# Product-key routing on Trainium2: the gates' exponentials on ACT, or as powers of e on POOL

## The chip, the cores and the metric

The kernel runs on one core of a Trainium2 chip. The metric is the time of one execution on the device, in microseconds (us); lower is better. The engines are named as in the profile: PE is the matrix engine (TensorE), PEld its weight load, DVE the vector engine, ACT the scalar engine, POOL GpSimd, SP the engine that issues most of the DMAs.

## The reference

Two blocks of a transformer work on 256 tokens of width 1024. The first block has two layers: latent attention and then chunked gated linear attention (`gla`), each followed by a feed-forward layer with product-key retrieval (`peer_ffn`). The second block is a token mixer and a hierarchical mixture of experts. The change lies in the retrieval layer:

```python
def one_block(xi):                                   # 128 tokens
    q = (xi @ w_query).reshape(B, T, 8, 2, 64)
    s = einsum('bthcd,cnd->bthcn', q, sub_keys)      # two halves, 128 keys each
    s_top, i_top = lax.top_k(s, 16)
    cand = s_top[..., 0, :, None] + s_top[..., 1, None, :]
    best, pos = lax.top_k(cand.reshape(..., 256), 16)
    idx = take_along_axis(cand_idx, pos)             # 16 of 16384 rows per head
    gate = softmax(best)
    h = gelu(einsum('bthkd,btd->bthk', u_tab[idx], xi))
    return einsum('bthk,bthkd->btd', gate * h, v_tab[idx])
```

Each token takes 16 rows for each of 8 heads, so 128 rows of `u` and 128 of `v` in each of the two layers. The gate is a softmax over the 16 best sums of a head.

## The kernel before

The program runs its stages one after the other: latent attention, the two retrieval layers with the linear attention between them (`experts`), the mixer, and the mixture of experts. Tiles, semaphores and the order of instructions on each engine are made when the program is built: a planner walks the instructions with a timeline of its own and puts each on its engine's queue when that timeline says it is ready. On the chip every engine works through its queue in that fixed order.

In `experts` there are four passes: layer 0 or 1 (`l`) and token block 0 or 1 (`b`). A pass has 128 gathers of 128 rows each (one row per token): one indirect DMA from POOL (L911) brings, for one of the token's 128 choices, the `u` row and the `v` row, 8 KB per token. Ten buffers (`g`) hold gathers. A slot of the loop is one gather and its work in `meet`: DVE multiplies the `u` half with the token's vector and sums (a dot into `hs`), and for two gathers together ACT takes gelu (L920), DVE multiplies with the gate, ACT makes a diagonal matrix for each (L924), and PE multiplies it with the `v` half into the output sums (L927); after that the buffer is free for a later gather.

The rows of a group of heads are chosen by `route`, whose steps are strewn between the slots of the group before: two matmuls against the keys, top-16 of each half on DVE, the candidate sums, top-16 again, the decoding of the row numbers (`idx`), and the gate. There are 17 groups: the first two have one head, the others two. In the pass of layer 0, block 1 and that of layer 1, block 0, the linear attention of the other token block (`gla`) is also worked in between the slots; it loads its own weights through SP, and takes exponentials, a logarithm and a silu on ACT.

All DVE instructions of `route` and the dots and gate products of `meet` are issued through the wrapper `InOrder` (line L135 in the profile for all of them), which adds a dependence from each to the one before. So they keep the order in which the program names them. DVE work of `gla` does not pass through the wrapper and can stand between.

The steps of the gate, at the end of `route`: DVE subtracts the best sum from all 16 (`gate`), ACT takes the exponential in place (L893), DVE sums it (`sm`), takes the reciprocal and multiplies. The next instruction on that chain is the next dot. ACT holds one table of functions at a time; the program has an ACT_TABLE_LOAD wherever the table changes, and the exponential and gelu are in different ones. Powers on POOL exist already in the kernel: the reciprocal root of each norm is taken as x to the power of -1/2 (`mhalf`, L300, L370, L651, L687 and others).

Of the kernel before, what the change touches and what calls it, by code (L numbers as in the profile page):

```python
# [9 lines left out]
FT = mybir.dt.float32  # L10
# [4 lines left out]
AF = mybir.ActivationFunctionType  # L15
OP = mybir.AluOpType
# [127 lines left out]
class K:  # L144
# [619 lines left out]
    def experts(self):  # L764
        nc, tc = self.nc, self.tc
        mm = nc.tensor.matmul
        y = self.y
        with self.phase("peer", ps=(6, 7), pq=(2, 3)) as mp:
            V = InOrder(tc, nc.vector)
            n_a = [16 // (a + 1) for a in range(16)]  # L770
            offs = np.concatenate([[0], np.cumsum(n_a)])
            NC = int(offs[-1])
            ct = mp.tile([128, 3, 16], FT, name="ct")
            for j in range(1, 16):
                nc.gpsimd.memset(ct[:, 0, j - 1:j], float(offs[j]))
# [51 lines left out]
            def route(l, b, hs):  # L827
                n = len(hs)
# [19 lines left out]
                V.tensor_tensor(dif, tif[:, :, :, 1:16], tif[:, :, :, 0:15], op=OP.subtract)  # L848
                cand = new("cand", NC)
                for a in range(8):  # L850
                    k = n_a[a]
                    V.tensor_tensor(cand[:, :, int(offs[a]):int(offs[a]) + k], top[:, :, 1, 0:k],
                                    top[:, :, 0, a:a + 1].to_broadcast([128, n, k]), op=OP.add)
                V.tensor_tensor(cand[:, :, int(offs[8]):NC], top[:, :, 0, 8:16],
                                top[:, :, 1, 0:1].to_broadcast([128, n, 8]), op=OP.add)
# [34 lines left out]

                sm, gate = new("sm", 1), new("gate", 16, bufs=3)
                V.tensor_tensor(gate, best, best[:, :, 0:1].to_broadcast([128, n, 16]), op=OP.subtract)
                nc.scalar.activation(gate, gate, AF.Exp)  # L893
                V.tensor_reduce(sm, gate, axis=AX.X, op=OP.add)
                V.reciprocal(sm, sm)
                V.tensor_tensor(gate, gate, sm.to_broadcast([128, n, 16]), op=OP.mult)
# [4 lines left out]
            def prepare(l, b, hs):  # L901
                for h in hs:
                    yield from query(l, b, h)
                yield from route(l, b, hs)
# [52 lines left out]
            for j, (l, b, hs) in enumerate(groups):  # L957
# [3 lines left out]
                for _ in dots(batches):  # L961
# [7 lines left out]
                    while plan and slot >= plan[0][0]:  # L969
# [3 lines left out]
                        n = (slot - begin) * parts // max(1, end - begin)  # L973
# [350 lines left out]
    def moe(self, out):  # L1324
        nc, tc = self.nc, self.tc
        y = self.y
        with self.phase("moe", ps=(2, 3, 6, 7)) as mp:
# [134 lines left out]
            def experts(once):  # L1462
                wts = weights(once)
                for q in range(8):
# [58 lines left out]
                    for b in range(2):  # L1523
                        for n in range(2):
                            mm(y[b][n], C[:, b, :], ys[:, n * 512:(n + 1) * 512], start=False, stop=False,
                               skip_group_check=True)

            experts(True)
            fin = self.pp.tile([128, 2, 1024], FT, name="fin", tag="h")
            sq1 = fin[:, 1, 512:640]  # L1530
# [11 lines left out]
            with tc.For_i(1, rounds, 1):  # L1542
                nc.vector.tensor_scalar(rank, rank, -32.0, None, op0=OP.add)
                experts(False)
# [39 lines left out]
```

## Time and profile before

| | before |
|---|---|
| median of 3 runs | 2353.03 us (2347.0 to 2353.46) |
| the profiled execution | 2348.37 us |
| its span, first to last instruction | 2346.6 us |
| mean granted clock of PE in it | 0.966 |
| busy in the span: PE, DVE, ACT, POOL | 2041.3, 1416.9, 714.4, 637.2 us |
| DMA | 849.30 MB, mean 362 GB/s |

The page of the profile gives these sums for the whole span; the stages have different limits, so the windows by stage say more. A line of a group gives the busy time, the mean duration, and the idle time of that engine just before these instructions with what ended it. In a timeline, the bracket at the end of a line is that idle time for one instruction.

### The profile page before, as it was taken

What the parts mean: (1) busy time and instruction counts of PE and PEld (TensorE: products, weight loads), DVE (VectorE), ACT (ScalarE), POOL (GpSimd) and SP (SyncE); (2) the same over time, 40 slices, a digit from 0 to 9 for tenths busy, and PEclk for the clock granted to TensorE, in tenths of its full rate; (3) what the DMA queues carried; (4) which work ended last, traced back from release to release, by engine and by line L of the source; (5) the groups of instructions that cost most, each with busy time, mean ns of one, the idle gap of its engine ahead of it and who ended that gap; (6) DMA issues with size and microseconds to landing.
All of it is one profiled execution on the core that took longest, in us unless ns stands there. A gap on an engine that the chain in (4) does not pass through costs nothing. (4 is left out here: it accounts for less than half of the span.)

```text
span 2346.6 us, 26348 instructions
## 1 busy us (share of the span) xinstructions
PE 2041.3 (87%) x8134; PEld 1068.5 (46%) x8136; DVE 1416.9 (60%) x3813; ACT 714.4 (30%) x1767; POOL 637.2 (27%) x666
## 2 busy tenths in 40 slices
PE   8999877879898888988887777779999989999996
PEld 7775333334444434444443232338899942222221
DVE  7768767778778678768787677556676530000001
ACT  6632222234344224344322222125555410000000
POOL 4124434434434443435344443410000000000000
PEclk9989999999999999999999999999999999999998
DMA  4359999999999999999999999965477699999996
GB/s 157 101 209 401 419 421 421 421 421 421 422 399 388 395 421 421 422 421 420 378 421 421 421 421 421 421 254 173 150 244 252 231 385 417 417 418 417 418 418 278
DMA packets 161210, 849.30 MB, mean 362 GB/s; under 512 B 18308, under 2 KB 18948, under 8 KB 95528
## 3 DMA queue, kind: packets, MB, share of 16 engines
q0 software_dynamic: 73728, 536.90, 55.4%
q1 hardware_dynamic: 87048, 310.12, 34.3%
q8 instruction: 68, 1.11, 0.2%
q14 instruction: 78, 0.64, 0.1%
q10 hardware_dynamic: 288, 0.52, 0.1%
HBM read 846.42 MB, written 1.05 MB: 361 GB/s over the span
## 5 line engine op out<-in xcount | busy, mean ns | idle before, releaser
L927 PE MATMUL ps<-g,dw 128*128 128x512 f32 x2048 | 976.7, 626 | 191.8 <-ACT dw L924 189.7
L911 POOL DMA_INDIRECT g<-in_puv_dram,idx x512 | 575.0, 1123 | 808.1 <-PE ps L927 466.8
L135 DVE CUSTOM_DVE_ANT_0 g<-g,xs 128x1024 f32<-128x1024 f32 x512 | 621.3, 1221 | 176.9 <-DMA g<-in_puv_dram,idx 164.4
L927 PEld LDWEIGHTS ps<-g,dw 128*128 128x128 f32 x2048 | 392.2, 199 | 720.9 <-issue 401.9
L270 DVE TENSOR_TENSOR wl<-raw,wh 128x512 fp32r<-128x512 f32 (+3 forms) x404 | 268.7, 678 | 128.7 <-ACT wh L268 114.2
L268 ACT ACTIVATE wh<-raw 128x512 fp32r<-128x512 f32 (+3 forms) x408 | 242.2, 613 | 135.2 <-PE ps L293 115.8
L920 ACT ACTIVATE w<-hs 128x2 f32<-128x2 f32 x256 | 51.9, 203 | 687.2 <-DVE hs L135 686.9
L1499 PE MATMUL ps<-we,xT 128*32 128x512 f32 x788 | 185.2, 600 | 20.3 <-DMA we<-in_e_gu_dram 20.3
L924 ACT ACTIVATE dw<-ident,w 128x128 f32<-128x128 f32 x512 | 177.4, 393 | 61.6 <-DVE w L135 57.3
L1504 DVE TENSOR_TENSOR hid<-hid,ps 128x512 f32<-128x512 f32 x8 | 5.5, 687 | 246.1 <-PE ps L1499 246.1
L292 PE MATMUL ps<-xH,wh 128*128 128x256 f32 (+1 forms) x456 | 130.6, 286 | 1.1 <-DVE sel L1191 1.1
L294 PE MATMUL ps<-xL,wh 128*128 128x256 f32 (+1 forms) x456 | 130.6, 286 | 0.0
L293 PE MATMUL ps<-xH,wl 128*128 128x256 f32 (+1 forms) x456 | 130.2, 285 | 0.0
L1533 POOL MEMSET fin<- 128x128 f32 x1 | 0.2, 206 | 404.0 <-DMA we<-in_e_gu_dram 404.0
L1499 PEld LDWEIGHTS ps<-we,xT 128*32 128x32 f32 x788 | 35.7, 108 | 159.7 <-DMA we<-in_e_gu_dram 116.1
L1517 PE MATMUL ps<-we,hT 128*32 128x512 f32 x400 | 95.4, 598 | 0.1
L135 DVE TENSOR_TENSOR w<-w,gate 128x2 f32<-128x2 f32 x256 | 41.1, 160 | 87.5 <-ACT w L920 82.5
L292 PEld LDWEIGHTS ps<-xH,wh 128*128 128x128 f32 (+1 forms) x456 | 87.2, 191 | 2.9 <-issue 1.5
L294 PEld LDWEIGHTS ps<-xL,wh 128*128 128x128 f32 (+1 forms) x456 | 87.2, 191 | 1.2 <-issue 1.1
L293 PEld LDWEIGHTS ps<-xH,wl 128*128 128x128 f32 (+1 forms) x456 | 87.3, 191 | 0.7 <-issue 0.6
L292 PE MATMUL ps<-wh,x 128*128 128x512 f32 (+1 forms) x160 | 63.9, 400 | 16.5 <-ACT wh L268 16.1
L294 PE MATMUL ps<-wl,x 128*128 128x512 f32 (+1 forms) x160 | 68.7, 431 | 7.2 <-DVE wl L270 6.3
(452 smaller groups left out, 2438.5 us busy)
## 6 DMA issues: line engine op xcount, KB each, us to landing
we<-in_e_gu_dram SPq DMA_DIRECT2D x197, 512.0 KB
we<-in_e_dn_dram SPq DMA_DIRECT2D x100, 512.0 KB
raw<-in_gla_w_dram SPq DMA_DIRECT2D x48, 512.0 KB
wx<-in_e_gu_dram SPq DMA_DIRECT2D x35, 512.0 KB
raw<-in_pq_dram SPq DMA_DIRECT2D x24, 512.0 KB
raw<-in_mx_conv_dram SPq DMA_DIRECT2D x24, 512.0 KB
raw<-in_e_gu_dram SPq DMA_DIRECT2D x24, 512.0 KB
g<-in_puv_dram,idx POOLq DMA_INDIRECT x512
```

The costliest lines, as they stand in the source:

```text
L135: r = f(*a, **k)
L268: nc.scalar.activation(H[:, :n], src, AF.Copy)
L270: e.tensor_tensor(L[:, :n], src, H[:, :n].bitcast(FT), op=OP.subtract)
L292: mm(out, aH, bH, start=start, stop=False, **kw)
L293: mm(out, aL, bH, start=False, stop=False, **kw)
L294: mm(out, aH, bL, start=False, stop=stop, **kw)
L911: nc.gpsimd.indirect_dma_start(out=g.rearrange("p a b -> p (a b)"), out_offset=None, in_=self.i[f"puv{l}"], in_offset=bass.IndirectOffsetO ...
L920: nc.scalar.activation(w, hs, AF.Gelu)
L924: nc.scalar.activation(d, self.ident, AF.Copy, scale=w[:, k:k + 1])
L927: mm(y[b][n], d, g[:, 1, n * 512:(n + 1) * 512], start=False, stop=left[l, b] == 0, skip_group_check=True)
L1499: mm(p[e * 32:(e + 1) * 32, :], xg[:, c, e * 32:(e + 1) * 32], ws[e][:, u * 512:(u + 1) * 512], start=c == 0, stop=c == 7, skip_group_chec ...
L1517: mm(pd[n][e * 32:(e + 1) * 32, :], hT[:, c, e * 32:(e + 1) * 32], ws[e][:, n * 512:(n + 1) * 512], start=c == 0, stop=c == 3, skip_group_ ...
```

## The change

In `experts`, a tile of one column is filled with e, once. In `route`, the exponential of the gate is no longer an activation on ACT but a two-input operation on POOL: the constant, spread over the tile, to the power of the gate's input. Nothing else is edited; the gelu, and the exponentials, logarithm and silu of `gla`, stay on ACT.

```diff
@@ in experts
             NC = int(offs[-1])
+            self.euler = mp.tile([128, 1], FT, name="euler")
+            nc.gpsimd.memset(self.euler, math.e)
             ct = mp.tile([128, 3, 16], FT, name="ct")
@@ in route
                 V.tensor_tensor(gate, best, best[:, :, 0:1].to_broadcast([128, n, 16]), op=OP.subtract)
-                nc.scalar.activation(gate, gate, AF.Exp)
+                nc.gpsimd.tensor_tensor(gate, self.euler[:, :, None].to_broadcast([128, n, 16]), gate, op=OP.pow)
                 V.tensor_reduce(sm, gate, axis=AX.X, op=OP.add)
```

## Rows read from the trace of the kernel before

**Rows 1.** The changed line, all its instructions.

```profile
L893 ACT ACTIVATE gate<-gate x17: 215/229/231, 151.4 to 1455.0; 128x32 f32<-128x32 f32 x15, 128x16 f32<-128x16 f32 x2
```

**Rows 2.** The routing stage: PE, PEld, DVE, ACT, POOL busy, PEclk, DMA share, GB/s.

```profile
150.00:1550.00 1400.00, 1167.54 (x3136) 550.41 (x3134) 1035.89 (x2755) 432.34 (x1150) 587.13 (x527) 0.95 1.00 414
```

**Rows 3.** Windows around single gates, the same columns.

```profile
225.00:230.00 5.00, 5.00 (x13) 2.28 (x12) 4.46 (x9) 1.79 (x6) 2.59 (x3) 1.00 0.67 224
...
545.00:565.00 20.00, 17.58 (x55) 9.52 (x54) 17.51 (x44) 10.00 (x22) 8.37 (x7) 1.00 1.02 423
...
740.00:760.00 20.00, 17.25 (x56) 9.77 (x56) 18.31 (x40) 10.99 (x27) 8.42 (x6) 0.91 1.00 407
...
1120.00:1140.00 20.00, 15.12 (x33) 6.45 (x32) 16.61 (x37) 8.66 (x19) 5.47 (x5) 0.74 0.79 314
```

**Rows 4.** Groups of DVE in the window 150 to 1550.

```profile
L135 DVE CUSTOM_DVE_ANT_0 g<-g,xs 128x1024 f32<-128x1024 f32 x506 | 613.9, 1221 | 169.4 <-DMA g<-in_puv_dram,idx 159.2 <-PE ps L927 8.2 <-issue 0.8
...
L135 DVE TENSOR_REDUCE sm<-gate 128x2 f32<-128x32 f32 (+1 forms) x17 | 3.1, 184 | 9.2 <-ACT gate L893 9.2
```

**Rows 5.** The gathers' DMA queue on the page (packets, MB, share).

```profile
q0 software_dynamic: 73728, 536.90, 55.4%
```

**Rows 6.** Groups of ACT in the window 150 to 1550.

```profile
L920 ACT ACT_TABLE_LOAD x23 | 29.5, 1283 | 0.4
L893 ACT ACT_TABLE_LOAD x16 | 20.5, 1283 | 0.3
```

**Rows 7.** DVE in order of time (start, duration, instruction, idle before it).

```profile
159.31 1.22 DVE L135 CUSTOM_DVE_ANT_0 g<-g,xs 128x1024 f32<-128x1024 f32 x1
...
221.38 0.18 DVE L135 TENSOR_REDUCE sm<-gate 128x2 f32<-128x32 f32 x1 [3.99 <-ACT gate L893]
...
293.96 0.18 DVE L135 TENSOR_REDUCE sm<-gate 128x2 f32<-128x32 f32 x1 [0.30 <-ACT gate L893]
...
301.28 1.23 DVE L135 CUSTOM_DVE_ANT_0 g<-g,xs 128x1024 f32<-128x1024 f32 x1 [1.16 <-DMA g<-in_puv_dram,idx]
...
1125.86 0.18 DVE L135 TENSOR_REDUCE sm<-gate 128x2 f32<-128x32 f32 x1 [0.72 <-ACT gate L893]
```

**Rows 8.** ACT in order of time.

```profile
289.00 1.28 ACT L893 ACT_TABLE_LOAD   x1
...
293.94 1.28 ACT L920 ACT_TABLE_LOAD   x1
```

**Rows 9.** Groups of POOL in the whole span, by shape.

```profile
L300 POOL TENSOR_TENSOR gst<-gst,mhalf 128x1 f32<-128x1 f32 x8 | 6.9, 864 | 11.0 <-DVE gst L299 10.4 <-DVE w L135 0.6
L651 POOL TENSOR_TENSOR rk<-ss,mhalf 128x16 f32<-128x16 f32 x2 | 5.8, 2922 | 0.1
...
L687 POOL TENSOR_TENSOR rq<-rq,mhalf 128x8 f32<-128x8 f32 x2 | 3.3, 1632 | 0.0
...
L575 POOL TENSOR_TENSOR t<-kr,tabs 128x32 f32<-128x32 f32 x1 | 0.3, 300 | 1.9 <-DVE kr L611 1.9
```

**Rows 10.** Durations of one POOL power (ns: shortest, median, longest).

```profile
L300 POOL TENSOR_TENSOR gst<-gst,mhalf x8: 550/562/1595, 650.0 to 1087.9; 128x1 f32<-128x1 f32 x8
```

**Rows 11.** POOL in order of time.

```profile
152.21 1.23 POOL L911 DMA_INDIRECT g<-in_puv_dram,idx  x1 [20.45 <-DVE gate L135]
...
300.66 0.94 POOL L911 DMA_INDIRECT g<-in_puv_dram,idx  x1 [7.01 <-PE ps L927]
...
556.05 0.95 POOL L911 DMA_INDIRECT g<-in_puv_dram,idx  x1 [9.01 <-DVE hs L135]
...
1135.15 1.27 POOL L911 DMA_INDIRECT g<-in_puv_dram,idx  x1 [11.40 <-PE ps L927]
```

**Rows 12.** L911 alone (POOL) in a window from 150 us.

```profile
150.00:300.60 150.60, 65.96 (x60) 0.93 0.97 399
```

**Rows 13.** Instructions that touch `xs` (PE, PEld, DVE) in that window.

```profile
150.00:300.60 150.60, 0.00 (x0) 0.00 (x0) 66.61 (x55) 0.93 0.97 399
```

**Rows 14.** PE in order of time.

```profile
456.98 3.56 PE L927 MATMUL ps<-g,dw 128*128 128x512 f32 x4 [2.37 <-ACT dw L924]
```

## The prediction, on record before the change was run

> **What bounds the kernel now.** I read the page first, then the windows by stage, then the groups of DVE, ACT and POOL for the routing stage alone, and last the timelines around single gates. The changed line runs 17 times, from 151 to 1455 us of the span [rows 1], all of it in the product-key stage, which lasts from about 150 to 1550 us. There no engine is full: in those 1400 us PE is busy 1168, DVE 1036, POOL 587 and ACT 432, while the DMA share is 1.00 and the rate 414 GB/s [rows 2]; full windows show 420 to 423, as the one from 545 [rows 3]. DVE's dot products wait 159.2 us for gathers to land [rows 4]. So DMA sets this stage: 536.90 MB in 512 gathers [rows 5] are 1.049 MB each, which at 421 GB/s take 2.49 us. The rest of the span is not touched by the edit and moves with the end of this stage. Two questions follow. Relief on ACT buys little where ACT is 31% busy; and any new stop costs only what it starves DMA of.
>
> **What is removed.** On ACT the 17 exponentials at 0.23 us (3.9 us) go, and the 16 table loads of that line at 1.283 us (20.5 us) [rows 6]. With them go those loads of the gelu line that only undo them: 23 loads stand there now; the chunked-attention work behind (exponentials, logarithm, silu in both passes) still forces some 8 or 9 of them, so I take 14 away, 18 us. ACT gets back about 42 us. What of it lies on a path? DVE waited for the gate's exponential 9.2 us in the 17 gates together [rows 4], 3.99 of it at 217, and 0.30 at a quiet gate like that of 293 [rows 7]: the load runs at 289.00, while ACT waits for the gate's input, and the one back to gelu at 293.94 [rows 8], while DVE is at the rest of the gate and the next dot. Outside 217, 645 and 1124 ACT's part is hidden already. I give the relief 1 us.
>
> **What is added.** A POOL power of 128x32 for 15 groups and of 128x16 for the first two. The trace has powers on POOL, of another base and exponent: 128x1 takes 0.55 us undisturbed, 128x8 1.63 us, 128x16 2.92 us [rows 9, 10]. That is a line: (2.92 - 1.63) / 8 = 0.16 us for each column on a base of 0.37 us. So 128x16 costs 2.9 us and 128x32 5.5 us (estimate from that line). The lower bound is the POOL product of 128x32, 0.30 us [rows 9]: it would hold if a power with base e ran like a product. The upper bound takes the same line with the worst disturbance seen of a 128x1 power, 1.60 against 0.55 us [rows 10], so about 6.5 us. I take 5.5, since the rows of the same operation are nearest. The memset of the one-column constant runs once, while POOL waits for the first route.
>
> [...]
>
> **Where it stands in the order.** The routing chain and the dots are issued on DVE through one in-order wrapper, so the sum of the gates (`sm`) and every dot behind it wait for POOL, and nothing of the chain can pass. The wait of 0.30 us becomes about 5.5: **+5.2 us at a full gate**, +2.7 at the two half ones. Added up, 15 x 5.5 + 2 x 2.9 - 9.2 = 79 us of DVE standing still. That is the top of the cost, if none is hidden.
>
> POOL itself loses little: after a full gate it now stands idle about 7 us, waiting for PE to free a gather buffer (7.01 before 300.66 [rows 11]; seven of the eight quiet gates show 6.3 to 7.1), because those buffers need dots that come after the gate. The power fits in that hole. At most one gather of 0.9 to 1.3 us runs ahead of it. So what is late next is the following dot, then gelu, the diagonal, PE's matmuls, the freed buffer, and so the next gather.
>
> **What hides it.** Gathers already issued. At 300.66, when POOL resumes after the gate of 293.7, 60 gathers were issued and 55 dots begun; the 56th dot starts at 301.28 on its landing [rows 7, 12, 13]. The last of the 60 lands 4 transfers later, and a gather in its turn would show its dot at 301.28 + 5 x 2.49 = 313.73. A gather needs 7.1 us from issue to dot (the very first: 152.21 to 159.31) [rows 7, 11], so the one issued at 300.66 could show it at 307.8. The cover is 6.0 us. The same sum at the other seven quiet gates (374, 454, 830 and the four after 1200) gives 4.5 to 6.9. So in these eight groups +5.2 us is just about covered. [...] 6.0 against covers of 4.5 to 6.9 loses about 0.4 each: **3 us**.
>
> The six groups that share the stage with chunked attention (549, 645, 747, 924, 1019, 1124) have its weights in the DMA queues too, so I go by stops of POOL. A stop of 9.01 us before 556 leaves the 20 us window full (423 GB/s), and so does one of the same kind at 924; the one of 11.40 us before 1135 leaves 314, a loss of 20 x (1 - 314/421) = 5.1 us [rows 3, 11]. At 549 and 924 the stop grows to about 14 us: beyond 9, all of 5.2 would be lost, but by the row at 1135 less; half, 2.6 each. At 1124 the sum starts at 1125.86 [rows 7], about 2 us after the gate's input, so +3.4, all lost. At 747 DMA is under full already (407 GB/s) [rows 3]: 5.2. At 645, with a wait like that at 1124 and a full window, 1; at 1019, where POOL stops for 5 us only, nothing. Together **15 us**.
>
> At the start: DMA has nothing else until the first gather at 152.21 [rows 11]; the power (2.9 us) becomes ready just before it, at 151.4 [rows 1], and may go ahead of gathers: 2 us. The group at 217 waits 4.0 us already [rows 7], so +1.5, and right behind it DMA drops to 224 GB/s [rows 3]. **3.5 us**.
>
> **The sum.** 3 + 15 + 3.5 - 1 = 20.5 us. The profiled run took 2348.37 us (span 2346.6 and 1.8 around it), so 2369. The median of the runs shown is 2353.03, 4.7 above it: **2373 us**, +0.9%.
>
> **Rivals.** (1) *All of it is hidden*: the covers are 6 us and the stand 5.2, gathers in flight at the gla groups are more than I think; then the 3.5 us of the start and the ACT relief of 1 remain: 2350 to 2360, about 2355. For it: full windows at 9 us stops. Against: 11.40 us is not full, and stops of 7.1 become 12.3. (2) *Nothing is hidden* from the gla groups on: DVE is 74% and PE 83% busy [rows 2] and must make up 5.2 us each time, PE at half clock after each stand; up to the 79 us, so 2390 to 2432. Against: the dots' 159 us of waits for DMA are slack. (3) *Faster, the power is cheap*: at 0.3 us the DVE waits don't grow and the long waits for ACT (4.0 us at 217 [rows 7], some 2 at 645 and 1124) shrink; with the gelu loads out of the gla groups 6 to 9 us: 2345. It decides where a 128x32 power stays under about 1 us; three sizes of power speak against it. [...] (4) *POOL's ring drains*: the power is put in POOL's order ahead of gathers whose buffers are free, and waits there for DVE as well. Against: the eight powers of L300 that POOL runs among the gathers wait 11.0 us at the head of its order in all [rows 9], 1.4 each. At 6 us beyond the cover for each gate, 17 x 6 = 102 us: 2455.
>
> **How the numbers follow.** Forecast (partly hidden, 2360 to 2385) 0.58; hidden 0.17; nothing hidden 0.14; cheap or faster 0.08; drained ring 0.03. No change is within 0.3%, 7 us, about the spread of the three runs before (6.5 us). Faster 0.08, same 0.16, slower 0.76. The range leaves out the drained ring, most of the unhidden case above 2402 and the fastest case: 2349 to 2402.
>
> **What would show it.** A 128x32 power of 5.5 us on POOL 15 times; DVE's wait of `sm` for POOL at about 85 us in total, from 9.2 for ACT; POOL's stops after a gate about 12 us instead of 7, with the power inside; table loads of the gelu line down to 8 or 9; DMA under 400 GB/s near 549, 747, 924 and 1124, and full in the quiet groups; the first mixer instruction some 20 us later and the span behind it unchanged. Wrong if the power is under 1 us, if quiet groups lose several us each, or if the scheduler moves gathers from one side of the gate to the other.

## The result, and the profile after

The change makes the kernel slower: a median of 2386.74 us (2383.68 to 2388.03) against 2351.88 us (2347.0 to 2353.46) for the kernel before, four runs each. The ratio is 1.0148, with an interval from 1.0135 to 1.0161, so +34.9 us. The forecast was +20 us (2373, range 2349 to 2402): right in its sign and its mechanism, 14 us short in size. The time lies inside the range, and 2 us above the band from 2360 to 2385 that was thought the likeliest.

The profiled execution took 2386.14 us, at a granted clock of 0.952. In the changed kernel the line numbers are two higher: L895 is the power, L913 the gather, L922 gelu, L929 the matmuls. From the page (span; busy time of each engine; the costliest group of DVE):

```profile
span 2384.4 us, 26316 instructions
...
PE 2039.7 (86%) x8134; PEld 1073.7 (45%) x8136; DVE 1413.5 (59%) x3813; ACT 672.5 (28%) x1719; POOL 736.6 (31%) x684
...
L135 DVE CUSTOM_DVE_ANT_0 g<-g,xs 128x1024 f32<-128x1024 f32 x512 | 619.8, 1220 | 131.7 <-DMA g<-in_puv_dram,idx 122.0
```

ACT is busy 42 us less and POOL 99 us more, as the edit would have it, and DVE and PE have the work they had. Yet the span is 37.8 us longer (3 us of that arise in its first 35 us, where both kernels issue the same instructions, and stay out of the account). The first and last gather show where it is: they start at 152.2 and 1544.4 us before, at 155.2 and 1582.8 after. From the last gather to the end it is 802 us in both. So some 35 us are lost between the first and the last gather, and nothing behind it.

The added line itself (shortest, median, longest duration in ns; first and last start):

```profile
L895 POOL TENSOR_TENSOR gate<-euler,gate x17: 2931/5447/5824, 157.7 to 1493.8; 128x32 f32<-128x32 f32 x15, 128x16 f32<-128x16 f32 x2
```

5.45 us for 128x32 and 2.93 for 128x16: the straight line through the kernel's other powers [rows 9] gave 5.5 and 2.9.

DVE's waits over 150 to 1640 us (waiting instruction, releaser: total us, times, longest):

```profile
DVE g L135 <- DMA g<-in_puv_dram,idx: 122.0, 143, 2.1
DVE w L135 <- ACT w L922: 101.6, 236, 5.4
DVE sm L135 <- POOL gate L895: 76.1, 16, 7.4
```

The same three waits in the kernel before, over the same window:

```profile
DVE g L135 <- DMA g<-in_puv_dram,idx: 164.4, 191, 2.0
DVE w L135 <- ACT w L920: 82.5, 228, 7.6
DVE sm L135 <- ACT gate L893: 9.2, 17, 4.0
```

This is the account of the change in three lines. The wait for the gate's power grew by 67 us. The dots' wait for DMA, the slack of the chain, shrank by 42. And the gate product's wait for gelu grew by 19, of which 18 came in the two stretches shared with the linear attention (480 to 765 and 845 to 1190 before): some gelus there stand in ACT's order behind a step of the linear attention that waits for PE. 67 - 42 + 19 = 44, near the 35 that the stage lost.

One quiet gate on DVE, in order of time; it answers to the gate at 293.94 of [rows 7]:

```profile
300.80 0.18 DVE L135 TENSOR_TENSOR gate<-best 128x32 f32<-128x32 f32 x1
...
306.55 0.19 DVE L135 TENSOR_REDUCE sm<-gate 128x2 f32<-128x32 f32 x1 [5.57 <-POOL gate L895]
...
318.76 1.23 DVE L135 CUSTOM_DVE_ANT_0 g<-g,xs 128x1024 f32<-128x1024 f32 x1 [0.50 <-DMA g<-in_puv_dram,idx]
```

And on POOL, which answers to the stop before 300.66 of [rows 11]:

```profile
301.07 5.45 POOL L895 TENSOR_TENSOR gate<-euler,gate 128x32 f32<-128x32 f32 x1 [1.42 <-DVE gate L135]
306.71 1.01 POOL L913 DMA_INDIRECT g<-in_puv_dram,idx  x1 [0.19 <-issue]
313.36 1.30 POOL L913 DMA_INDIRECT g<-in_puv_dram,idx  x1 [5.65 <-PE ps L929]
```

DVE stands 5.57 us where it stood 0.30. The dots behind then catch up with the gathers that have landed meanwhile; the first that waits for DMA again starts at 318.76, 12 us after the gate. POOL's idle stretch of 7.01 us has become 1.42, the power, one gather, and 5.65 more in which it waits for PE to free a buffer.

Windows over the stage, behind this gate, behind another quiet one (860 to 880), and behind the gates of the groups shared with the linear attention (PE, PEld, DVE, ACT, POOL busy, clock, DMA share, GB/s):

```profile
300.00:320.00 20.00, 10.69 (x18) 4.59 (x19) 12.68 (x30) 3.70 (x12) 10.26 (x6) 0.74 1.01 420
...
565.00:585.00 20.00, 17.61 (x38) 7.97 (x38) 14.16 (x35) 5.00 (x15) 11.25 (x8) 0.84 0.92 357
665.00:685.00 20.00, 17.91 (x46) 8.54 (x46) 13.11 (x35) 7.78 (x18) 10.55 (x8) 0.95 1.02 421
760.00:780.00 20.00, 13.80 (x59) 9.56 (x59) 11.40 (x24) 5.26 (x17) 9.37 (x5) 0.83 0.60 235
860.00:880.00 20.00, 20.00 (x46) 8.75 (x45) 15.17 (x41) 4.68 (x15) 13.25 (x12) 0.96 0.92 358
945.00:965.00 20.00, 14.74 (x35) 6.86 (x34) 14.01 (x30) 6.66 (x20) 9.86 (x7) 0.91 0.96 370
1040.00:1060.00 20.00, 13.75 (x34) 7.39 (x34) 10.93 (x24) 7.31 (x15) 9.53 (x5) 0.83 1.02 422
1080.00:1120.00 40.00, 31.94 (x82) 14.35 (x80) 29.36 (x82) 16.28 (x43) 13.13 (x13) 0.83 0.87 348
1160.00:1180.00 20.00, 14.81 (x32) 6.46 (x31) 16.46 (x34) 8.09 (x23) 10.98 (x8) 0.78 0.68 257
...
150.00:1590.00 1440.00, 1171.33 (x3166) 559.95 (x3165) 1035.47 (x2762) 392.10 (x1105) 686.55 (x544) 0.93 0.98 401
```

The quiet gate of 300 is covered: the gathers in flight keep DMA at 420 GB/s while DVE stands. Not every quiet gate is: where the forecast had DMA full, 20 us run at 388 GB/s from 390, 396 from 470, 358 from 860, 346 from 1260 and 389 from 1410. Of the seven windows beside the linear attention, five fall short. Against 421 GB/s, 20 us at 235 lose 8.8 us, at 257 7.8, at 357 3.0, at 370 2.4, and the 40 us at 348 lose 6.9: together 29, of which some 6 were lost at these places before (5.1 of them behind the gate at 1124 [rows 3]).

A group can still make up for what a window loses. What is lost for good shows from gate to gate, from one subtraction on DVE to the next. Before, the gate at 1019 and the one behind it:

```profile
1018.70 0.18 DVE L135 TENSOR_TENSOR gate<-best 128x32 f32<-128x32 f32 x1
...
1123.51 0.24 DVE L135 TENSOR_TENSOR gate<-best 128x32 f32<-128x32 f32 x1
```

and the same two after:

```profile
1039.37 0.18 DVE L135 TENSOR_TENSOR gate<-best 128x32 f32<-128x32 f32 x1
...
1156.88 0.18 DVE L135 TENSOR_TENSOR gate<-best 128x32 f32<-128x32 f32 x1
```

104.8 us have become 117.5, so 12.7 us are lost behind this one gate. The same difference is 0.3, 1.2, 5.0, 3.2 and 3.2 us behind the other five that share the stage with the linear attention (549, 645, 747, 924 and 1124), 5.5 us behind the eight quiet gates together, and 4.4 behind the three at the start. These are single executions: in the run below with the power in the quiet groups alone, the six other groups still differ from before by up to 1.6 us.

### The profile page after: what moved, and what is told of

The parts are those of the page before. It is cut to its first block, busy times and chain, and to the rows that moved or that the text cites. A ratio compares the mean times of both kernels' runs of the same rounds, so it can differ in the third digit from the quotient of the medians.

```text
span 2384.4 us, 26316 instructions
## 1 busy us (share of the span) xinstructions
PE 2039.7 (86%) x8134; PEld 1073.7 (45%) x8136; DVE 1413.5 (59%) x3813; ACT 672.5 (28%) x1719; POOL 736.6 (31%) x684
## 5 line engine op out<-in xcount | busy, mean ns | idle before, releaser
L929 PE MATMUL ps<-g,dw 128*128 128x512 f32 x2048 | 975.0, 627 | 225.1 <-ACT dw L926 223.7
L913 POOL DMA_INDIRECT g<-in_puv_dram,idx x512 | 585.9, 1144 | 730.9 <-PE ps L929 446.5
L929 PEld LDWEIGHTS ps<-g,dw 128*128 128x128 f32 x2048 | 396.9, 200 | 752.1 <-issue 413.8
L135 DVE CUSTOM_DVE_ANT_0 g<-g,xs 128x1024 f32<-128x1024 f32 x512 | 619.8, 1220 | 131.7 <-DMA g<-in_puv_dram,idx 122.0
L270 DVE TENSOR_TENSOR wl<-raw,wh 128x512 fp32r<-128x512 f32 (+3 forms) x404 | 268.4, 678 | 123.9 <-ACT wh L268 115.4
L922 ACT ACTIVATE w<-hs 128x2 f32<-128x2 f32 x256 | 51.9, 203 | 785.0 <-DVE hs L135 784.9
L895 POOL TENSOR_TENSOR gate<-euler,gate 128x32 f32<-128x32 f32 (+1 forms) x17 | 88.9, 5232 | 8.6 <-DVE gate L135 8.1
```

What stands on the lines that cost most here:

```text
L135: r = f(*a, **k)
L270: e.tensor_tensor(L[:, :n], src, H[:, :n].bitcast(FT), op=OP.subtract)
L895: nc.gpsimd.tensor_tensor(gate, self.euler[:, :, None].to_broadcast([128, n, 16]), gate, op=OP.pow)
L913: nc.gpsimd.indirect_dma_start(out=g.rearrange("p a b -> p (a b)"), out_offset=None, in_=self.i[f"puv{l}"], in_offset=bass.IndirectOffsetO ...
L929: mm(y[b][n], d, g[:, 1, n * 512:(n + 1) * 512], start=False, stop=left[l, b] == 0, skip_group_check=True)
```

## The experiments

Three theories were set against each other. **A**: the in-order chain on DVE stands for as long as the power runs, less what the gathers in flight cover. **B**: POOL, busy with the power, issues its gathers late. **C**: with the power on POOL, the planner puts other work in another order, and that costs. Times are medians; "before" is the kernel before, run beside these on the same chip (2351.01, 2351.77 and 2351.82 us in the three sets).

**A cheap operation in the same place.** In most groups the order stays nearly the same and only the duration goes.

```diff
-nc.gpsimd.tensor_tensor(gate, self.euler[...], gate, op=OP.pow)
+nc.gpsimd.tensor_tensor(gate, self.euler[...], gate, op=OP.mult)
```

> The power is replaced by a product with the same constant at the same place on POOL, so the exponential is left out and the gates are other numbers; waits, queues and ACT's relief stay. Theory A (DVE's in-order chain stands still for as long as the power runs): the stand falls from 5.6 to about 0.4 us a gate, and the time returns to that of before, 2346 to 2358 us. Theory B (POOL is occupied between gathers): the same, 2346 to 2358. Theory C (the planner's new order costs time whatever the power takes, above all in the tails of the linear attention at 1080 to 1120 us of the changed kernel): 2360 to 2372.

Measured: 2354.58 us, ratio 1.0005 (0.9987 to 1.0024). The cost is gone, so it hangs on the duration of the power and not on the engine or the semaphore. C falls for most groups, but not for all: with a cheap operation to place, the planner goes back to about the order of the kernel before behind the gates at 645 and 1019. Behind the one at 1019, 3 of DVE's 210 instructions stand elsewhere than in the kernel before, and 35 elsewhere than in the changed kernel. There this run takes away the power's duration and the new order together. Its profiled execution alone lost some 17 us ahead of the first gather, so its span isn't used; from the first gather to the last it took 1398.9 us (1392.2 before, 1427.6 in the changed kernel). DVE's wait for POOL in it:

```profile
DVE sm L135 <- POOL gate L895: 17.0, 15, 3.6
```

**The same power, earlier on the chain.** The gate needs only `best`, so subtraction and power can be issued ahead of the decoding of the row numbers (some 6.4 us of DVE work on the chain, with dots between), and `sm` stays where it was.

```diff
+                sm, gate = new("sm", 1), new("gate", 16, bufs=3)
+                V.tensor_tensor(gate, best, ..., op=OP.subtract)
+                nc.gpsimd.tensor_tensor(gate, self.euler[...], gate, op=OP.pow)
                 posf, red, row = new("posf", 16), new("red", 16), new("row", 16)
...
                 V.tensor_copy(idx, row)
-                sm, gate = new("sm", 1), new("gate", 16, bufs=3)
-                V.tensor_tensor(gate, best, ..., op=OP.subtract)
-                nc.gpsimd.tensor_tensor(gate, self.euler[...], gate, op=OP.pow)
                 V.tensor_reduce(sm, gate, axis=AX.X, op=OP.add)
```

> The changed kernel with the gate's difference and the power moved ahead of the decoding of the row numbers, so that some 7 us of DVE work and the dots between lie under the power; the sum of the gates stays where it was. Theory A: no stand is left, DVE waits under 15 us in total for the power (76.1 now), time 2346 to 2360. Theory B: POOL is occupied as long as before, so 2375 to 2390. Theory C: 2360 to 2372.

Measured: 2347.73 us, ratio 0.998 (0.9962 to 0.9998), with a power as long as before (5.38 us in the mean of the 17). POOL is as occupied as in the changed kernel, if earlier, so B falls with this run. Its waits of DVE:

```profile
DVE g L135 <- DMA g<-in_puv_dram,idx: 179.1, 209, 2.3
...
DVE sm L135 <- POOL gate L871: 2.1, 1, 2.1
```

The wait of 76.1 us is down to 2.1, and the dots wait for DMA again, 179.1 us, more than before the change.

**A power that nobody reads.** The kernel before, with the power added on POOL behind each gate.

```diff
                 V.tensor_tensor(gate, gate, sm.to_broadcast([128, n, 16]), op=OP.mult)
+                again = new("again", 16)
+                nc.gpsimd.tensor_tensor(again, self.euler[...], gate, op=OP.pow)
```

> The kernel before, exponential on ACT, and beside it a power of the same shape on POOL behind each gate, into a tile that nobody reads. Theory A: POOL's power fits in its wait for PE, and nothing waits for it: 2350 to 2360. Theory B: POOL's occupation is the cost: 2375 to 2390. Theory C: between, as the order is changed, 2350 to 2370.

Measured: 2356.65 us, ratio 1.0016 (0.9999 to 1.0033). So 17 powers on POOL, 5.8 us each in the mean, cost 4 to 6 us (up to 8 by the interval) when nothing waits for them. B is at best a small part. DVE's wait for the exponential on ACT rose in this kernel, from 9.2 us, so not all of it need be POOL's:

```profile
DVE sm L135 <- ACT gate L895: 18.7, 17, 4.0
```

**The stand without POOL.** The kernel before, with 8 products of 128x480 (4 at the half gates) added to DVE's chain at each gate. The eight take 5.51 us at the gate of 299.56.

```diff
                 nc.scalar.activation(gate, gate, AF.Exp)
+                for _ in range(8 if n == 2 else 4):
+                    V.tensor_tensor(prod, cmp, dif[...].to_broadcast(big), op=OP.mult)
```

> The kernel before, exponential on ACT, and behind it 8 more products of 128x480 on DVE's in-order chain at each full gate (4 of 128x240 at the two half ones), some 5.3 us (1.7 us), into a scratch tile: the stand without POOL. Theory A: about the loss of the change, 2372 to 2390. Theory B: POOL is free, so 2350 to 2362. Theory C: little, 2350 to 2365.

Measured: 2378.08 us, ratio 1.0105 (1.0058 to 1.0152), +27 us (14 to 36 by the interval) with no power at the gates at all. Here too the dots' wait for DMA shrank:

```profile
DVE g L135 <- DMA g<-in_puv_dram,idx: 136.2, 157, 2.3
```

So by the median the stand of the chain is most of the cost, whatever makes it. 8 us of the 35 aren't reproduced; what they are is taken up below.

**Two powers in a row**, the first of them into a tile that nobody reads.

```diff
+                again = new("again", 16)
+                nc.gpsimd.tensor_tensor(again, self.euler[...], gate, op=OP.pow)
                 nc.gpsimd.tensor_tensor(gate, self.euler[...], gate, op=OP.pow)
```

> The changed kernel with a second power of the same shape right ahead of the first, into a scratch tile: the stand of DVE at a full gate goes from 5.6 to about 11 us. Theory A (the stand, less the cover of issued gathers, which the first 5.6 us have used up): each further microsecond is lost nearly whole, 15 x 5.4 + 2 x 2.9 = 87 us at most, so 2450 to 2475. Rival (the loss grows as the stand does, 35 us for the first 5.3): 2418 to 2430.

Measured: 2462.74 us, ratio 1.047 (1.0443 to 1.0497), +111 us. The second power at each gate (5.4 us, 2.9 at the two half ones) cost 76 us, 4.5 for each gate: where the first has used the cover up, nearly all is lost.

```profile
DVE g L135 <- DMA g<-in_puv_dram,idx: 117.4, 134, 2.5
...
DVE sm L135 <- POOL gate L897: 154.4, 16, 12.2
```

The wait for `sm` doubled from 76.1 to 154.4, while the dots' slack gave only 5 us more (122.0 to 117.4).

**Relief on ACT alone.** The kernel before with a copy in place of the exponential; no table load stands at its line in the trace, where the exponential had 16.

```diff
-                nc.scalar.activation(gate, gate, AF.Exp)
+                nc.scalar.activation(gate, gate, AF.Copy)
```

> The kernel before with a copy on ACT in place of the exponential, so the exponential is left out and the gates are other numbers, and the table loads around it fall away: ACT's relief alone, same engine, same place. Theory A: the loads were hidden, 2346 to 2352 us. Rival (the relief is worth what DVE waited, 9.2 us at the gates and part of 82 us for gelu): 2335 to 2344.

Measured: 2348.10 us, ratio 0.9984 (0.9974 to 0.9993): 3.7 us for all the table loads saved. The loads left are those of the changed kernel:

```profile
L920 ACT ACT_TABLE_LOAD x8 | 10.3, 1283 | 0.1
```

**The power in some groups only**, the exponential on ACT in the others. First the six groups that share the stage with the linear attention:

```diff
+                if l != b and hs[0]:
                     nc.gpsimd.tensor_tensor(gate, self.euler[...], gate, op=OP.pow)
+                else:
+                    nc.scalar.activation(gate, gate, AF.Exp)
```

> The power on POOL only in the six groups that share the stage with the linear attention; the other eleven keep the exponential on ACT. By the prediction's terms 15 us, so about 2367; by the delays of the dots in the changed kernel about 22 us, so 2370 to 2378. If the quiet groups carry the loss, 2350 to 2358.

Measured: 2377.69 us, ratio 1.0107 (1.009 to 1.0123): +26 us from six gates, 4.3 each in the mean. In its profiled execution, 32 us longer than before from the first gather to the last, 13.1 us lie behind the gate that stood at 1019 before, and the order of DVE's and ACT's instructions behind that gate is exactly the changed kernel's.

Then the eight quiet groups:

```diff
+                if (l == b and (l or hs[0] > 2)) or (l != b and hs[0] == 0):
                     nc.gpsimd.tensor_tensor(gate, self.euler[...], gate, op=OP.pow)
+                else:
+                    nc.scalar.activation(gate, gate, AF.Exp)
```

> The power on POOL only in the eight quiet groups; the other nine keep the exponential on ACT. By the prediction's terms 3 us, so 2354 to 2356; by the delays of the dots in the changed kernel about 7 us, 2357 to 2361. If the quiet groups carry the loss, 2370 to 2378.

Measured: 2357.92 us, ratio 1.0029 (1.0018 to 1.004): +6 us from eight gates, 0.8 each. DVE's wait for POOL in it:

```profile
DVE sm L135 <- POOL gate L896: 47.9, 8, 7.2
```

48 us of DVE standing cost 6: the other 42 lay beside transfers. The two runs add up to 32 of the 35 us, which leaves about 3 for the three gates at the start, within the noise of three medians. From gate to gate the changed kernel's own execution says the same: 25.5, 5.5 and 4.4.

**Half the power**, for the first head of a group only (128x16).

```diff
-nc.gpsimd.tensor_tensor(gate, self.euler[...].to_broadcast([128, n, 16]), gate, op=OP.pow)
+nc.gpsimd.tensor_tensor(gate[:, 0:1], self.euler[...].to_broadcast([128, 1, 16]), gate[:, 0:1], op=OP.pow)
```

> The changed kernel with the power of the first head of each group alone, 128x16, about 2.9 us in all 17 groups (the second head's gates stay without exponential, other numbers): the stand at a full gate is about 3.0 us instead of 5.6. Theory A (stand, with a cover that differs by group): the quiet groups hide it, the linear-attention groups lose 2.7 each, 2362 to 2372. Rival (loss in proportion to the stand, no cover): 2387 less 15 x 2.5, so 2345 to 2351.

Measured: 2363.85 us, ratio 1.0062 (1.004 to 1.0084), +12 us, with a wait for `sm` of

```profile
DVE sm L135 <- POOL gate L895: 40.3, 14, 4.8
```

Powers of 2.9, 5.4 and twice 5.4 us cost 12, 35 and 111 us: the price rises faster than the stand, as it would where a fixed cover is used up first.

**The exponential on ACT, earlier.** The three lines moved as in the early power, in the kernel before.

```diff
+                sm, gate = new("sm", 1), new("gate", 16, bufs=3)
+                V.tensor_tensor(gate, best, ..., op=OP.subtract)
+                nc.scalar.activation(gate, gate, AF.Exp)
                 posf, red, row = new("posf", 16), new("red", 16), new("row", 16)
...
                 V.tensor_copy(idx, row)
-                sm, gate = new("sm", 1), new("gate", 16, bufs=3)
-                V.tensor_tensor(gate, best, ..., op=OP.subtract)
-                nc.scalar.activation(gate, gate, AF.Exp)
```

> The kernel before with the gate's difference and the exponential, still on ACT, moved ahead of the decoding of the row numbers, as the early power was. Theory A (what the early power gained is ACT's relief, 3 to 4 us): no gain here, 2349 to 2354. Rival (the gain is that DVE no longer waits 9.2 us at the gates): 2345 to 2349.

Measured: 2350.92 us, ratio 0.9991 (0.9981 to 1.0001): the 9.2 us that DVE waited for ACT before were worth 1 us, at most 4 to 5 by the interval. The gain of the early power, if there is one, isn't the move itself.

**The early power again**, in five rounds, to see whether it beats the kernel before.

> The early power once more, in more rounds, beside the early exponential: 2346 to 2350 by theory A, 0.1 to 0.3 per cent under the kernel before.

Measured: 2348.29 us, ratio 0.999 (0.9976 to 1.0004). Both runs lie below the kernel before, by 0.1 and 0.2%, in the size of the relief on ACT (3.7 us); the second can't be told from no change.

## Why the prediction was right, and where its size was off

**The power's price: right.** 5.5 us from the line through three smaller powers, 5.45 measured. From 128x16 to 128x32 it is 0.16 us for a column ((5.45 - 2.93) / 16), as in the forecast's line. The cheap-power rival, which needed less than about 1 us, ends here.

**The stand: right.** DVE's wait for `sm` was forecast at about 85 us in place of 9.2; it is 76.1, and part of the stands beside the linear attention is filled with its weight splits (3.74 us of L270 in the one that ends at 767.10). The chain behind it is the cause of most of the loss: the product, the early power and DVE's own stand show it from three sides.

**The quiet groups: right in kind, 3 us forecast, 6 measured.** The cover of 4.5 to 6.9 us hides most of each stand, but not all: 300 to 320 us stays at 420 GB/s, 860 to 880 falls to 358. The stand was to be 5.2 us longer; in the run with these eight powers alone it is 47.9 us, 6.0 for each gate. The extra is consistent with single gates where the stand was longer than the power, since a gather ran ahead of it on POOL: the longest wait of `sm` is 7.4 us, at 470, behind the gate that stood at 454 before (the gather starts at 463.43, the power at 464.40). "At most one gather of 0.9 to 1.3 us runs ahead" was in the text, but not in the sum. The forecast had 6.0 us against the covers too, but as the stand of 5.2 and 0.8 for PE behind it, and no run shows these 0.8 us. What the trace shows of PE behind the gate at 300 in their place: it is idle up to 309.31, a matmul of L929 takes 1.06 us from 310 to 314.5, at a granted clock of 0.50, and 0.59 from 320 to 325, at 1.00; before, the four of a gather took 3.56 us at 457 [rows 14].

**The linear-attention groups: the step that failed, 15 us forecast, 26 measured.** "So I go by stops of POOL", and by that rule one term above all: "at 1019, where POOL stops for 5 us only, nothing". From gate to gate 12.7 us were lost there. The other five gates lost 12.8 us together where 14.8 was forecast: 0.3, 1.2, 5.0, 3.2 and 3.2 against 2.6, 1, 5.2, 2.6 and 3.4. That this sum came out so near is in part luck, since next to nothing was lost at 549.

POOL's stop measures how long no gather is issued, not how much slack the dots behind have. That slack was to be read from DVE. The group of dots in the kernel before, in the quiet stretch 235 to 480 and in the stretch with linear attention 480 to 765 (count; busy us, mean ns; idle us before them and what ended it):

```profile
L135 DVE CUSTOM_DVE_ANT_0 g<-g,xs 128x1024 f32<-128x1024 f32 x98 | 119.7, 1224 | 49.0 <-DMA g<-in_puv_dram,idx 46.8 <-PE ps L927 1.4 <-issue 0.6
...
L135 DVE CUSTOM_DVE_ANT_0 g<-g,xs 128x1024 f32<-128x1024 f32 x92 | 111.5, 1217 | 11.9 <-DMA g<-in_puv_dram,idx 11.7
...
L135 DVE TENSOR_TENSOR w<-w,gate 128x2 f32<-128x2 f32 x45 | 7.2, 159 | 12.3 <-ACT w L920 12.3
```

A quiet dot waits 0.48 us for its gather on average, one beside the linear attention 0.13. DMA is all but full there too (409 GB/s from 480 to 765, with the linear attention's weights beside the gathers), but the gathers land ahead of their dots, so a chain that is late has little to take back. The same stretch after (490 to 785):

```profile
L135 DVE CUSTOM_DVE_ANT_0 g<-g,xs 128x1024 f32<-128x1024 f32 x92 | 111.4, 1215 | 6.5 <-DMA g<-in_puv_dram,idx 5.5 <-PE ps L929 0.8
...
L135 DVE TENSOR_TENSOR w<-w,gate 128x2 f32<-128x2 f32 x45 | 7.2, 160 | 19.5 <-ACT w L922 19.4
```

Only 6 us of slack could be taken back in three gates, and 7 us of waits for gelu came on top. The forecast used one sum of 159 us of slack for the whole stage [rows 4]; in the six groups that cost most there were, in the two stretches, 11.7 and 11.8 us of it. By single gates the difference is plainer: behind the gate at 549 the dots had 4.5 us of such waits before and hardly anything was lost, and behind the one at 1019 no dot waited for DMA at all.

What the chain on DVE waits for behind that gate in the changed kernel:

```profile
1045.50 0.19 DVE L135 TENSOR_REDUCE sm<-gate 128x2 f32<-128x32 f32 x1 [4.70 <-POOL gate L895]
...
1057.44 0.16 DVE L135 TENSOR_TENSOR w<-w,gate 128x2 f32<-128x2 f32 x1 [3.05 <-ACT w L922]
...
1080.58 0.29 DVE L135 MAX8 top<-sc 128x8 f32<-128x128 f32 x1 [5.84 <-ACT sc L837]
...
1101.44 0.16 DVE L135 TENSOR_TENSOR w<-w,gate 128x2 f32<-128x2 f32 x1 [5.04 <-ACT w L922]
```

Only the first is the power. The third is for scores of the next routing, whose matmuls come late on PE; the other two are for gelus that stand in ACT's order behind a step of the linear attention (L1088), which waits 1.17 and 4.61 us for PE and has a table load on either side. Before, the longest wait of the chain in this group was one of 1.90 us for gelu. DMA holds at 422 GB/s up to 1060, and then loses 6.9 us from 1080 to 1120, a stretch that ran full before (420 GB/s from 1060 to 1100). How much of this the stand brings, and how much the order that the planner chose around the power, no run separates. With DVE's own stand, as long but in yet another order, the group lost 5.4 us; with the power in the six groups alone, in the same order, 13.1; with the product, in about the order of the kernel before, 2.1.

At 747 the loss came out as forecast, 5.0 us, but not surely for the reason given: the product still lost 3.6 us there, and the stand was longer than forecast. On DVE:

```profile
758.02 3.74 DVE L270 TENSOR_TENSOR wl<-raw,wh 128x512 fp32r<-128x512 f32 x6
767.10 0.19 DVE L135 TENSOR_REDUCE sm<-gate 128x2 f32<-128x32 f32 x1 [5.35 <-POOL gate L895]
```

and POOL:

```profile
760.18 1.14 POOL L913 DMA_INDIRECT g<-in_puv_dram,idx  x1 [2.25 <-PE ps L294]
761.35 5.72 POOL L895 TENSOR_TENSOR gate<-euler,gate 128x32 f32<-128x32 f32 x1
```

The gate's input is done at 758.1, but POOL's order has a gather ahead of the power, and that gather waits until 760.18 for its buffer. The chain stands 9.0 us, not 5.5.

**The start: 3.5 forecast, about 3 left over** from the two split runs, 4.4 from gate to gate. The first power does go ahead of a gather, as feared (157.72, between the second and the third).

**The relief on ACT: 1 us forecast, 3.7 measured** with the copy. The gelu line's table loads fell to 8, as forecast, and 42 us of ACT's busy time with it; the 3.7 us lie inside the 35.

**What stays open.** DVE's own stand cost 27 us and the power 35, though the power also brings the relief on ACT, so 8 to 12 us are left. From gate to gate 7 of them lie behind the gate at 1019 (12.7 us with the power, 5.4 with DVE's own stand), where the two kernels have different orders. No run has the changed kernel's order there with a short operation, so theory C stays open for these 7 us. The rest can be gathers kept waiting on POOL (4 to 6 by the power that nobody reads) and stands made longer by a gather ahead of the power (7.4 us at the gate of 454, 9.0 at that of 747). These were not told apart.

## What to carry to other kernels

Moving a short operation to a slower idle engine was priced here by what waited in order behind its result (76.1 us of DVE's waits), not by the busy shares of the two engines (28% and 31%); if its input is ready early, issue it early: the slow engine then cost nothing (2347.73 us with the same power, 2386.74 without the move). Read the slack that is to hide a delay separately for each stretch, from the waits of the instruction just behind it (0.48 us a dot in one, 0.13 in the other, none behind the gate that cost most): a sum over the stage puts slack where there is none. Where a planner orders the work, compare the orders too before a duration is blamed. And a cover is used up once: powers of 2.9, 5.4 and twice 5.4 us cost 12, 35 and 111 us.

## What the runs showed of the hardware

A POOL power of e to a tensor cost here what a power with a fixed exponent did: 2.93 us for 128x16 where that took 2.92 [rows 9]. For 128x32 it took 5.45, while the product in its place took 0.24 us in the mean of the 17 (4.0 us of POOL together). Removing 31 table loads of 1.283 us each, 40 us of ACT's time, gave back 3.7 us. And PE's granted clock was lower in the executions with long stands of the chain: in the mean 0.966 before, 0.955 with DVE's own stand, 0.952 with the power and 0.939 with two. Behind the gate at 300 it is 0.74 over 20 us: PE stands idle there for 9.43 us up to 309.31, runs at 0.50 from 310 to 315, and from 315 to 320 is back at 0.96. In the changed kernel a window of 5 us at 0.50 stands behind each of the eight quiet gates.
